# Seven products in place of eight for the gate and up projections of a SwiGLU block

## The chip, the cores and the metric

The kernel runs on one core of a Trainium2 chip. The metric is the device time of one execution in microseconds; the time of a kernel is the median of its runs. Each kernel also leaves one profiled execution, taken by the hardware profiler.

Engines by the names that the profile uses: PE is the matrix engine (PEld its weight loads), DVE the vector engine, ACT the scalar engine, POOL GpSimd, and SP the engine on whose queue the DMAs are issued. SBUF is the memory on the chip with 128 partitions, PSUM the eight banks of 128 x 512 floats into which PE accumulates, DRAM the memory outside.

## The reference

One layer of a bidirectional encoder on two sequences (prompt and sample) of 256 tokens each, so T = 512 columns in all, with a model width of 2048 and a feed-forward width of 5632, in float32:

```
hn = rms_norm(x, norm1_g) * (1 + sc1) + sh1          # sh, sc, gt: from silu(c) @ w_ada
h  = hn @ w_in                                       # RWKV-7 heads and a short convolution
x  = x + gt1 * (concat([y_rwkv, y_conv]) @ w_out)
hn = rms_norm(x, norm2_g) * (1 + sc2) + sh2
ff = (silu(hn @ w_ffn_gate) * (hn @ w_ffn_up)) @ w_ffn_down
y  = rms_norm(x + gt2 * ff, norm_f_g)
```

The change concerns the last three lines. sh2, sc2 and gt2 are vectors of 2048 for each of the two sequences; they come from a product of silu(c) with w_ada (2048 x 12288), which the kernel computes piece by piece beside other work.

## The kernel before

Everything is kept transposed: a row tile is 128 channels on the partitions and the 512 tokens as columns, the prompt in columns 0 to 255 and the sample in 256 to 511. KT = 16 row tiles make the model width, FT = 44 column tiles the feed-forward width.

**Precision.** A float32 product is made of three matmuls on a faster rounded format (fp32r): a weight is split into a high part (rounded, by ACT, `acopy`) and a low part (the rest, by DVE, `tt` with subtract), an activation likewise, and high x high, high x low and low x high are accumulated. `products` (L529) issues the three, `split` (L511) makes 512 columns of high and low weights, four 128 x 128 blocks, into one of four ring slots h. `load` (L522) brings 512 KB of raw weights (eight blocks) into one of three slots w. `stream` (L536) walks a list of tiles in this way, and `mtile` (L557) lists the products for one output tile of 512 columns in one bank.

**Order.** The code does not issue its instructions in the order written. `Program.add` records each operation with its engine, an estimated cost, what it reads and writes, and a priority; `Program.schedule` (L239) then plans the whole kernel, engine by engine, always taking the ready operation of the lowest priority number, and the instructions are issued in the planned order. Each engine's queue then runs strictly in that order, SP's DMA queue included. Priorities that matter here: 0 for weight splits (S_SPLIT), 1 for evacuations and most DMAs (S_EVAC), 5 for other side work (S_MISC), 8 for w_ada work (S_ADA), 9 for the large products (S_MAIN). Buffers are named slots: r0 to r15, g0 to g23, w0 to w2, h0 to h3, aw and aacc, each of 1024 columns. An operation that writes a slot under a new name waits for all earlier uses of it.

**The FFN.** After the out projection, `halves` (L1104) finishes its last four row tiles for the prompt columns first and then for the sample, so that the norm of one half runs beside the products of the other. `hn2_half` (L1174) makes the normalized activations hn2 of one row tile and one sequence, as high and low parts. The first three gate and up tiles run together over all row tiles (`head_tiles`), with their first four row tiles done by halves of 256 columns, their weights kept in six slots. Then for each further tile f, gate and up run as 16 x 3 matmuls of 512 columns each; `gate_done` applies silu from PSUM, `up_done` (L1208) multiplies and splits the result into one of twelve slots av. As soon as eleven activations (FCH) are there, the down projection adds their share to all 16 row tiles (four chunks, NCH): `down_done` (L1234) adds gt2 times the product to the residual x1 in SBUF. So gate, up and down alternate in four rounds:

```
nf = 3
for c in range(NCH):
    while nf < min(FCH * (c + 1) + 1, FT):
        for j in range(2):
            b0 = 2 * (2 * (nf - 3) + j)
            stream(lambda i, b0=b0: w_gu1[b0 + i],
                   mtile(hn2, next_bank(5), (gate_done, up_done)[j](nf)))
        nf += 1
```

The last four row tiles of the last chunk go by halves again, followed by the final norm.

**w_ada.** `ada_rest` (L758) brings one group of 512 columns of w_ada, in one of two ways. With slots it uses PE; without, it loads sixteen 256 KB pieces into the two halves of aw, and DVE multiplies and accumulates them into aacc (two operations of 512 columns each), before eight small matmuls sum over the partitions. Groups 12 to 15 (ADA_LATE), which give gt2, go the second way, written after the norm of the FFN.

## Time and profile before

| what | before |
| --- | --- |
| time, median of 3 runs | 2552.27 us (2551.53 to 2554.98) |
| profiled execution | 2558.41 us, span 2556.2 us |
| PE busy | 2493.4 us, 15340 matmuls |
| DVE busy | 1467.7 us, 2807 instructions |
| ACT busy | 969.8 us, 1764 instructions |
| DMA | 352.73 MB, 138 GB/s over the span |

The span runs from the first to the last instruction of the profiled execution; its whole time is a little longer. Matmuls are pipelined, and the duration of one matmul in the profile is longer than the distance to the next, so the rate is read from the starts in the timeline. Rows of the timeline give start, length, engine, line, operation, output and inputs by the program's names, and the count; idle time before the row and what ended it stand in square brackets. Rows of groups give busy time in us and the mean of one in ns after the first bar, idle time just before them and its causes after the second. The rows of 40 digits are busy tenths of 40 equal slices of the span.

### The profile page before, as it was taken

How to read it: one execution, taken by the hardware profiler on the slowest of the kernel's cores; microseconds unless marked ns; L12 is line 12 of the kernel's file. 1: busy time of each engine (PE TensorE's matmuls, PEld its weight loads, DVE VectorE, ACT ScalarE, POOL GpSimd, SP SyncE). 2: the span in 40 equal slices, each digit the busy share in tenths (PEclk: the TensorE clock that was granted, in tenths of full speed). 3: DMA queues.
4: the chain of work that ended last, by engine and by line, in shares of the span. 5: the costliest groups of instructions: out<-in, count | busy, mean ns of one | idle time of the engine just before them, and what ended most of it. 6: DMA issues, size and time to landing. Idle time of an engine off the chain costs nothing.

```text
span 2556.2 us, 39032 instructions
## 1 busy us (share of the span) xinstructions
PE 2493.4 (98%) x15340; PEld 1990.8 (78%) x15340; DVE 1467.7 (57%) x2807; ACT 969.8 (38%) x1764; POOL 12.5 (0%) x42
## 2 busy tenths in 40 slices
PE   6999999999999999999999999999999999999997
PEld 3578777777777777788788888888888888888887
DVE  4279988888988887888733333333333333333345
ACT  4474663754654732333222222222222222222232
POOL 0000000000000000000000000000000000000000
PEclk9999999999999999999999999999999999999999
DMA  9943443544544757636533333333333333333333
GB/s 347 362 145 122 145 135 113 147 130 128 154 132 126 239 185 266 206 124 191 182 98 99 91 99 99 94 96 99 93 97 99 99 93 98 99 93 98 99 93 105
DMA packets 147880, 352.73 MB, mean 138 GB/s; under 512 B 31856, under 2 KB 46576, under 8 KB 147696
## 3 DMA queue, kind: packets, MB, share of 16 engines
q1 hardware_dynamic: 147696, 350.24, 43.7%
q8 instruction: 120, 1.97, 0.3%
q14 instruction: 64, 0.52, 0.1%
HBM read 339.30 MB, written 12.45 MB: 138 GB/s over the span
## 4 chain that ended last, share of the span: by engine, by line
PE 82%; DVE 7%; DMA 6%; ACT 3%; issue 2%; SPq 1%; DVEq 0%; ACTq 0%
PE b L374 82%; DVE g L405 3%; DMA aw<-in_w_ada_dram 2%; ACT g L396 2%; DVE h L405 1%; DVE aacc L410 1%; DVE g L410 1%; DMA g<-hrmean 1%; SPq L438 1%; DMA g<-hrpre 1%; DMA w<-in_w_out_dram 0%; ACT h L396 0%; DVE r L410 0%; PE b L385 0%; ACT L396 0%
## 5 line engine op out<-in xcount | busy, mean ns | idle before, releaser
L374 PE MATMUL b<-r,h 128*128 128x512 f32 x4872 | 1187.6, 396 | 4.4 <-ACT r L396 1.9
L374 PEld LDWEIGHTS b<-r,h 128*128 128x128 f32 x4872 | 901.7, 189 | 223.8 <-issue 28.4
L374 PE MATMUL b<-g,h 128*128 128x512 f32 x4460 | 1045.0, 392 | 0.8 <-ACT g L396 0.5
L405 DVE TENSOR_TENSOR h<-w,h 128x512 fp32r<-128x512 f32 (+3 forms) x795 | 539.7, 680 | 784.1 <-ACT h L396 753.7
L374 PEld LDWEIGHTS b<-g,h 128*128 128x128 f32 x4460 | 836.1, 188 | 191.9 <-issue 11.2
L396 ACT ACTIVATE h<-w 128x512 fp32r<-128x512 f32 x787 | 492.8, 627 | 1237.9 <-PE b L374 1182.5
L410 DVE SCALAR_TENSOR_TENSOR aacc<-aw,sil,aacc 128x512 f32<-128x512 f32 x390 | 276.1, 744 | 60.1 <-DMA aw<-in_w_ada_dram 58.8
L405 DVE TENSOR_TENSOR g<-g,g 128x512 f32<-128x512 f32 (+24 forms) x699 | 255.9, 374 | 34.2 <-ACT g L396 12.2
L396 ACT ACTIVATE g<-b 32x128 f32<-32x128 f32 (+4 forms) x442 | 175.6, 402 | 133.1 <-PE b L374 101.3
L374 PEld LDWEIGHTS b<-g,g 128*64 128x64 f32 (+4 forms) x4104 | 158.8, 140 | 49.2 <-issue 27.2
L374 PE MATMUL b<-g,g 128*64 128x64 f32 (+4 forms) x4104 | 179.3, 229 | 4.4 <-DVE g L441 1.9
L396 ACT ACTIVATE g<-g 128x512 f32<-128x512 f32 (+3 forms) x190 | 113.7, 601 | 63.4 <-DVE g L405 52.3
L410 DVE SCALAR_TENSOR_TENSOR r<-b,md,r 128x256 f32<-128x256 f32 x192 | 84.9, 478 | 53.6 <-PE b L374 53.6
L405 DVE TENSOR_TENSOR g<-g,b 128x512 f32<-128x512 f32 x60 | 41.1, 685 | 59.4 <-PE b L374 59.3
L374 PE MATMUL b<-g,sil 128*32 128x512 f32 (+1 forms) x384 | 44.0, 554 | 21.0 <-DMA g<-in_w_ada_dram 19.1
L396 ACT ACT_TABLE_LOAD x45 | 57.7, 1283 | 1.5 <-PEq L1399 0.7
L405 DVE TENSOR_TENSOR g<-b,cs 64x256 f32<-64x256 f32 (+1 forms) x128 | 49.6, 416 | 1.8 <-PE b L374 0.2
L396 ACT ACTIVATE g<-r 128x512 f32<-128x512 f32 (+1 forms) x40 | 21.7, 543 | 49.5 <-DVE r L410 39.3
L374 PEld LDWEIGHTS b<-g,sil 128*32 128x32 f32 x384 | 9.3, 113 | 39.0 <-ACT g L396 17.6
L441 DVE STREAM_TRANSPOSE g<-g 128x512 f32<-128x512 f32 (+1 forms) x32 | 38.4, 1211 | 0.4
L396 ACT ACTIVATE g<-g,md 128x256 f32<-128x256 f32 (+1 forms) x48 | 25.1, 561 | 22.3 <-DVE md L405 12.7
L385 PE MATMUL b<-cs,g 128*128 128x128 f32 x160 | 23.0, 278 | 7.6 <-DVE g L405 6.4
(83 smaller groups left out, 559.4 us busy)
## 6 DMA issues: line engine op xcount, KB each, us to landing
w<-in_w_gu_dram SPq DMA_DIRECT2D x176, 512.0 KB
aw<-in_w_ada_dram SPq DMA_DIRECT2D x208, 256.0 KB
w<-in_w_in_dram SPq DMA_DIRECT2D x102, 512.0 KB
w<-in_w_down_dram SPq DMA_DIRECT2D x88, 512.0 KB
g<-in_w_ada_dram SPq DMA_DIRECT2D x80, 512.0 KB
w<-in_w_out_dram SPq DMA_DIRECT2D x32, 512.0 KB
g<-in_xT_dram SPq DMA_DIRECT2D x8, 512.0 KB
r<-in_xT_dram SPq DMA_DIRECT2D x16, 256.0 KB
```

Of the source, the lines that this page charges most:

```text
L374: return [nc.tensor.matmul(R(out), lhsT=R(l), rhs=R(r), start=start, stop=stop) for out, l, r, n, start, stop, one in mms]
L385: return [nc.tensor.transpose(R(out), R(i), R(idn)) for out, i, idn in items]
L396: lambda: nc.scalar.activation(out=R(out), in_=R(in_), func=func, scale=R(scale), bias=R(bias)),
L405: lambda: e.tensor_tensor(out=R(out), in0=R(a), in1=R(b), op=op), [a, b], [out], prio)
L410: lambda: e.scalar_tensor_tensor(out=R(out), in0=R(a), scalar=R(s), in1=R(b), op0=op0, op1=op1),
L438: add(eng, cost, lambda: e.dma_start(R(out), R(in_)), [in_, *after], [out], prio, nbytes=nbytes)
L441: add("dve", 0.37 if n == 256 else 0.05 + n / 560.0, lambda: nc.vector.transpose(R(out), R(in_)), [in_], [out], prio)
```

## The change

For the column tiles 4 to 43, gate and up are computed for pairs of column tiles (f, f + 1) and pairs of row tiles (x, y) at once. With the weights as a 2 x 2 block matrix (two column tiles by two row tiles) and the activations as another (two row tiles by two halves of 256 tokens), the 2 x 2 block product is made of seven block products instead of eight, by the Winograd form of Strassen's method. Each block product is again three fp32r matmuls, now of 256 columns.

- `make_u`, once for each of the eight pairs of row tiles, makes the four sums of activation blocks that the method needs, in place of the float32 copy of hn2 that `hn2_half` now also writes over x1, and splits them (four DVE operations of 256 columns, two of 512 and two of ACT), into slots ua and ub.
- `pair_weights` loads two pieces of 256 KB (four row tiles of two column tiles), forms four sums of weight blocks on DVE (512, 256 and 256 columns), and splits three plain blocks per row pair (768 columns) and the four sums (1024 columns). Its rings: four raw slots, two for the sums, two for each kind of part.
- `pair_products` runs this four times for a pair of column tiles and gate or up, with 42 matmuls each, into four banks: banks 4 to 7 for gate, 0 to 3 for up.
- `pair_sums` combines the seven results into the four output blocks (one ACT copy, five DVE operations of 256 columns and one of 512).
- The product of silu(gate) and up, two tiles at once, is stored to DRAM (actd). The down projection no longer alternates with gate and up, but comes as a stage of its own. Its four chunks load their eleven activations from DRAM and split them (`load_act`); the next chunk's are loaded while the current one runs.
- The residual x1 is stored to DRAM after the out projection (`save_x1`), because its slots are used for other things, and loaded again for the last chunk (`load_x1`). The down projection sums plainly (`acopy` for the first chunk, one DVE sum of 512 columns for the others), and gt2 and the residual are applied once at the end (`add_x1`).
- The late w_ada groups are written after the first chunk of down. Two slots (aw, aacc) take the place of g8 and g9 for the kept weights of the head.

```diff
     def out_done(m):
         def f(ps):
             gated_add(2, m)(ps)
+            save_x1(m)
             sumsq(x1[m], tmp(), sqa2, m == 0, S_EVAC)
...
     def hn2_half(k, q):
...
+        act(x1[k][:, s], t[:, s], AF.Identity, TQ, S_EVAC, bias=md[:, 3, k, q:q + 1])
...
-    for gi in ADA_LATE:
-        ada_rest(gi)
...
+    def make_u(j):
+        x, y = (x1[k] for k in rows_of(j))
+        b11, b12, b21, b22 = x[:, 0:TQ], x[:, TQ:T], y[:, 0:TQ], y[:, TQ:T]
+        tt(b11, b12, b11, ALU.subtract, TQ, S_MISC)
+        tt(b12, b22, b12, ALU.add, TQ, S_MISC)
+        tt(b22, b22, b11, ALU.add, TQ, S_MISC)
+        tt(b21, b21, b22, ALU.subtract, TQ, S_MISC)
+        for u, v in ((ua[j], x), (ub[j], y)):
+            acopy(u[:, 0:T], v, T, S_MISC)
+            tt(u[:, T:], v, u[:, 0:T].bitcast(F32), ALU.subtract, T, S_MISC)
...
+    ring_raw = ring(raws + [Slot.of["aw"]], F32)
+    ring_s = ring([Slot.of["aacc"], gs[23]], F32)
+    ring_parts = [ring(x) for x in (hls[0:2], hls[2:4], gs[16:18], r1s[14:16])]
...
+    def pair_weights(f, j, n):
+        x, y = ring_raw(), ring_s()
+        ha, la, hs, ls = (r() for r in ring_parts)
+        for a in range(2):
+            b = 2 * (2 * (f + 1 - a - 3) + j) + n // 2
+            dma(x[:, 512 * a:512 * a + 512], w_gu1[b][:, 512 * (n % 2):512 * (n % 2) + 512], 1 << 18, S_EVAC)
+        acopy(ha[:, 0:768], x[:, 256:1024], 768, S_SPLIT)
+        two256 = [128, 2, 256]
+        tt(y[:, 0:512].rearrange("p (a c) -> p a c", a=2), x[:, 0:256][:, None, :].to_broadcast(two256),
+           x[:, 256:768].rearrange("p (a c) -> p a c", a=2), ALU.subtract, 512, S_SPLIT)
+        tt(y[:, 512:768], x[:, 512:768], y[:, 0:256], ALU.subtract, 256, S_SPLIT)
+        tt(y[:, 768:1024], x[:, 768:1024], y[:, 512:768], ALU.subtract, 256, S_SPLIT)
+        acopy(hs, y, 1024, S_SPLIT)
+        tt(la[:, 0:768], x[:, 256:1024], ha[:, 0:768].bitcast(F32), ALU.subtract, 768, S_SPLIT)
+        tt(ls, y, hs.bitcast(F32), ALU.subtract, 1024, S_SPLIT)
...
+                    for (hi, lo), (ah, al), (b, c, end) in zip(ws[i][g_], xs, place[g_]):
+                        ps, stop = banks[b][:, TQ * c:TQ * c + TQ], bool(end) and k == KT // 2 - 1
+                        pe([(ps, hi, ah, TQ, k == 0 and b not in seen, False, True),
+                            (ps, hi, al, TQ, False, False, True), (ps, lo, ah, TQ, False, stop, True)], S_MAIN,
+                           after=[seen[b]] if k == 0 and b in seen else [])
...
+    for f in range(4, FT, 2):
+        pair_products(f, 0, bank[4:8])
+        pair_sums(bank[4:8], gate2)
+        act(gate2, gate2, AF.Silu, 2 * T, S_EVAC)
+        pair_products(f, 1, bank[0:4])
+        pair_sums(bank[0:4], up2)
+        tt(up2, up2, gate2, ALU.mult, 2 * T, S_EVAC)
+        for i in range(2):
+            dma(all_of(actd[f + i]), up2[:, T * i:T * i + T], 1 << 18, S_EVAC)
...
+    early = halves_of([Slot.of[n] for n in ("aw", "aacc")])
+    in_act, in_x1 = halves_of(r1s[14:16] + gs[16:17]), halves_of(gs[17:18] + by_pair[2 * FCH + 8:])
...
+    def load_act(c, i, after=()):
+        a = VT(place[c % 2][i], F32R).v()[:, 0:2 * T]
+        t = early.pop(0) if early else in_act[(FCH * c + i) % len(in_act)]
+        dma(t, all_of(actd[FCH * c + i]), 1 << 18, S_EVAC, after=after)
+        acopy(a[:, 0:T], t, T, S_EVAC)
+        tt(a[:, T:], t, a[:, 0:T].bitcast(F32), ALU.subtract, T, S_EVAC)
+        return a
...
     def down_done(c, m):
         def f(ps):
-            gated_add(5, m)(ps)
+            if c == 0:
+                acopy(x1[m], ps, T, S_EVAC)
+            else:
+                tt(x1[m], x1[m], ps, ALU.add, T, S_EVAC)
             if c == NCH - 1:
+                add_x1(m, 0, 2)
                 sumsq(x1[m], tmp(), sqa2, m == 0, S_EVAC)
+                load_x1(m + AHEAD, [x1[m]])
+            elif m < FCH:
+                coming.append(load_act(c + 1, m, [x1[m]]))
+            elif c == NCH - 2 and m >= KT - AHEAD:
+                load_x1(m - (KT - AHEAD), [x1[m]])
```

More of the change, by code (lines that the diff above doesn't have):

```diff
@@ L1102, in gated_half, with halves @@
         return f
-    def halves(blocks, acts, kind, tiles, last, slots, norm, at):
+    def halves(blocks, acts, done, tiles, last, slots, norm, at):
         kept = [VT(x, F32R).v() for x in slots]
@@ L1184, in norm2, with save_x1 @@
             hn2_half(k, q)
+    x1d = [Scratch(drp.tile([128, T], F32, name=f"x1d{m}")) for m in range(KT)]
+    def save_x1(m):
+        dma(all_of(x1d[m]), x1[m], 1 << 18, S_EVAC)
     at = {"i": 0}
@@ L1231, in hymba_layer_kernel, with ring, take @@
                 products(kept[i // 4][:, w:w + 128], kept[i // 4][:, 512 + w:640 + w], *t)
+    for j in range(KT // 2):
+        make_u(j)
     stream(lambda i: w_gu0[i], tiles, at=at)
+    for j in range(2):
+        stream(lambda i, j=j: w_gu1[2 * j + i], mtile(hn2, bank[j], (gate_done, up_done)[j](3)))
+    def ring(slots, dt=F32R):
+        v, n = [VT(s, dt).v() for s in slots], [0]
+        def take():
+            n[0] += 1
+            return v[(n[0] - 1) % len(v)]
+        return take
@@ new lines, in hymba_layer_kernel @@
+    raw0[:] = [VT(s).v() for s in raws]
+    tmpv = [VT(gs[i]).v() for i in (20, 21, 22)]
+    tmpq[:] = [tmpv[i // 2][:, T * (i % 2):T * (i % 2) + T] for i in range(6)]
+    sqa2 = VT(gs[23]).v()[:, T:]
+    bctr["n"] = 3
+    def load_act(c, i, after=()):
[5 more added lines that the diff above has]
+        return a
@@ new lines, in down_done, with down_half, f @@
+        return f
+    def down_half(m, q):
+        def f(ps):
+            s = slice(TQ * q, TQ * q + TQ)
+            tt(x1[m][:, s], x1[m][:, s], ps, ALU.add, TQ, S_EVAC)
+            add_x1(m, q, q + 1)
+            sumsq(x1[m][:, s], tmp()[:, s], sqa2[:, s], False, S_EVAC)
+            if q == 0:
+                load_x1(m + AHEAD, [x1[m][:, s]])
+        return f
+    acts = [load_act(0, i) for i in range(FCH)]
+    wide.update((n, VT(Slot.of[n]).v()) for n in ("aw", "aacc"))
+    for c in range(NCH):
+        tiles, last, coming = [], LAST_DOWN * (c + 1 == NCH), []
```

92 lines of the change are left out of this document (72 added, 20 removed).

## The prediction

> **What bounds the kernel now.** I read the page first, then the timeline of PE in the two FFN stages, then the timeline and groups of DVE and ACT there, then busy time by stretches. From the page: the span, TensorE and its granted clock, and the vector engine by slices.
>
> ```profile
> span 2556.2 us, 39032 instructions
> PE 2493.4 (98%) x15340; PEld 1990.8 (78%) x15340; DVE 1467.7 (57%) x2807; ACT 969.8 (38%) x1764; POOL 12.5 (0%) x42
> ...
> DVE  4279988888988887888733333333333333333345
> ...
> PEclk9999999999999999999999999999999999999999
> ```
>
> The chain of waits, in order of time, ends in one piece of TensorE work that covers the whole second half, followed by the last normalization on DVE:
>
> ```profile
> 1234.51 1306.48 PE b L374 x5885
> 2545.80 3.95 DVE g L410 x10
> ```
>
> So from 1234 us on nothing but the rate of matmuls sets the time. That rate comes from the timeline of TensorE in the gate and up stage (start, length, engine, line, operation, count); the next two rows are the same engine where the kernel before already multiplies by 256 columns instead of 512, first in the head of the FFN and then in the last chunk of the down projection:
>
> ```profile
> 1314.00 5.60 PE L374 MATMUL b<-r,h 128*128 128x512 f32 x24
> 1319.44 5.60 PE L374 MATMUL b<-g,h 128*128 128x512 f32 x24
> ...
> 1094.00 14.39 PE L374 MATMUL b<-r,g 128*128 128x256 f32 x120
> 1108.23 4.04 PE L374 MATMUL b<-r,h 128*128 128x512 f32 x17
> ...
> 2508.39 11.62 PE L374 MATMUL b<-g,r 128*128 128x256 f32 x96
> 2519.84 4.46 PE L374 MATMUL b<-g,g 128*128 128x256 f32 x36
> ```
>
> From start to start: 5.44 us for 24 is 226.7 ns for 512 columns; 14.23 us for 120 is 118.6 ns and 11.45 us for 96 is 119.3 ns for 256 columns. Half the columns thus cost 0.526 of the time, not 0.5. I take 119.3, since that stretch reads weights as they are split, as the new stage will.
>
> **The change: TensorE.** Per pair of row tiles, pair of column tiles and gate or up, the old code runs 8 block products of three matmuls over 256 columns, which it issues as 12 of 512. The new code runs 7 block products, 21 matmuls of 256. There are 20 pairs of column tiles (f = 4 to 42), two matrices and 8 pairs of row tiles: 320 units. Old: 320 x 12 x 226.7 ns = 870.5 us. New: 320 x 21 x 119.3 ns = 801.7 us. **Gain 68.8 us**, that is 1.72 us in each of 40 half pairs (21.76 us before, 20.04 us after). Of the 12.5% of columns saved, the shorter matmuls give back 4.6 points. With 118.6 ns it would be 73.5 us.
>
> A weight load now has to fit beside half as long a matmul. The busy time by stretches shows that it does, even with DVE full and the clock at 1.00:
>
> ```profile
> core 0: us, PE busy (x) PEld busy (x) DVE busy (x) ACT busy (x) POOL busy (x), PEclk, DMA share, GB/s
> 1094.00:1108.00 14.00, 14.00 (x122) 14.00 (x121) 14.00 (x37) 7.86 (x18) 0.00 (x0) 1.00 0.00 1
> ```
>
> The Trainium skill, TensorE: Matmul & The Clock Gate, section "The mechanism", speaks against this: weight loads are said to overlap running matmuls only where their row groups differ, and here all are 128 rows. The row disagrees: 120 loads and 120 matmuls went by at 118.6 ns a pair. What it would do to the time is a rival below.
>
> **DVE and ACT in the new stage.** Groups by shape, for the costs (count, busy us, mean ns), and two neighbouring starts in the timeline of DVE:
>
> ```profile
> L405 DVE TENSOR_TENSOR h<-w,h 128x512 fp32r<-128x512 f32 x403 | 278.6, 691 | 635.0 <-ACT h L396 612.4 <-PE b L374 22.6
> L396 ACT ACTIVATE h<-w 128x512 fp32r<-128x512 f32 x402 | 254.2, 632 | 781.1 <-PE b L374 777.6 <-issue 3.5
> ...
> L405 DVE TENSOR_TENSOR h<-w,h 128x256 fp32r<-128x256 f32 x8 | 3.3, 418 | 0.3 <-ACT h L396 0.2
> L396 ACT ACTIVATE h<-w 128x256 fp32r<-128x256 f32 x8 | 3.2, 406 | 0.0
> L405 DVE TENSOR_TENSOR g<-b,g 128x256 f32<-128x256 f32 x16 | 6.7, 416 | 4.0 <-PE b L374 4.0
> ...
> 1314.20 0.69 DVE L405 TENSOR_TENSOR g<-g,b 128x512 f32<-128x512 f32 x1 [1.59 <-PE b L374]
> 1314.80 0.68 DVE L405 TENSOR_TENSOR h<-w,h 128x512 fp32r<-128x512 f32 x1
> ```
>
> A tensor_tensor has 0.69 us at 512 columns and 0.42 at 256, so by their slope an estimate of 0.97 at 768 and 1.24 at 1024; followed by independent work the next one starts 0.09 us before the end (0.60 from start to start). ACT, in the same way: 0.86 at 768, 1.08 at 1024.
>
> pair_weights, once per eight weight blocks (two units, 42 x 119.3 ns = 5.01 us of TensorE): DVE 0.69 + 2 x 0.42 + 0.97 + 1.24 = 3.74 us; ACT 0.86 + 1.08 = 1.94 us. Four of these make a half pair: 14.96 us of DVE. pair_sums adds 5 x 0.42 + 0.69 = 2.77 us, the final product half of 1.24. So DVE takes **18.35 us of the 20.04** with nothing overlapped, and 15.97 with 0.09 off each of about 26.5 instructions: 80 to 92%. ACT: 7.76 + 0.4 + half of 1.08 = 8.7 us. Before, DVE was at 33% here, so the engine loses nearly all of its slack, but keeps enough. I cost it at nothing. The cover is depth: two sets of split weights are 10 us of matmuls, and the order lets DVE make the low part (0.97 us) while ACT rounds the sums (1.08 us). If that cover goes, see the second rival.
>
> **Loads.** A unit pair takes 512 KB in 5.01 us, 105 GB/s, as two DMAs of 2 KB rows; the stage before moved 98 GB/s:
>
> ```profile
> 1600.00:1800.00 200.00, 200.00 (x879) 164.75 (x878) 66.68 (x105) 52.39 (x84) 0.00 (x0) 1.00 0.33 98
> ...
> 1100.00:1200.00 100.00, 100.00 (x501) 83.53 (x501) 81.64 (x139) 32.25 (x55) 0.00 (x0) 1.00 0.54 167
> ```
>
> The second row holds many loads of the same 256 KB form (w_ada) at 167 GB/s for 0.54 of the DMA engines, the same 300 GB/s per full share as the first. The stores of activations add 13 GB/s, their reloads and x1 (60 x 256 KB over down's 64 tiles of 33 x 226.7 ns, 479 us) 33 GB/s. Four raw buffers give SP 15 us of lead. Nothing. What one DMA costs SP's queue, what one ACT write of 256 columns with a bias costs, and the longest wait in the chain for a 256 KB piece near here:
>
> ```profile
> L438 SPq DMA_DIRECT2D w<-in_w_gu_dram x128: 327/328/328, 1458.0 to 2391.6; - x128
> ...
> L396 ACT ACTIVATE r<-g,md 128x256 fp32r<-128x256 f32 x16 | 7.3, 501 | 12.3 <-DVE g L410 12.3
> ...
> 1218.23 4.34 DMA aw<-in_w_ada_dram
> ```
>
> **Start of the stage.** save_x1 puts 16 stores on SP's queue, each behind the sum it stores; behind them wait w_ada pieces and the first FFN weights. 32 more ACT writes of x1 (0.5 us each) lie behind the normalization, and make_u takes 8 x (4 x 0.42 + 2 x 0.69) = 24.5 us of DVE under some 87 us of matmuls (72 head tiles and 32 of f = 3, three matmuls each at 226.7 ns is 71 us, plus 17 of 256 columns). In exchange the four late w_ada groups leave this place. TensorE stalls here now:
>
> ```profile
> 1083.53 0.65 PE L374 MATMUL b<-aacc,cs 128*32 128x128 f32 x8 [2.68 <-DVE aacc L410]
> 1084.59 0.65 PE L374 MATMUL b<-aacc,cs 128*32 128x128 f32 x8 [0.41 <-DVE aacc L410]
> 1085.81 1.01 PE L374 MATMUL b<-cs,g 128*128 128x1 f32 x4 [0.57 <-DVE asum L441]
> 1087.78 0.58 PE L374 MATMUL b<-r,g 128*128 128x256 f32 x1 [0.96 <-ACT r L396]
> ...
> 1085.00:1090.00 5.00, 3.28 (x20) 2.67 (x12) 4.66 (x19) 1.48 (x5) 0.00 (x0) 0.50 0.32 107
> ```
>
> These 4.6 us of idling could go (-5), or the stores could delay what it waits for by as much as the 16 x 0.33 = 5.3 us of queue, with a colder clock after it (+8). I take 0, since its causes stay as they are.
>
> **The late w_ada groups** move into down chunks 0 to 2: 128 multiply-adds on DVE and 64 DMAs on SP. In order on DVE they wait for their DMAs, and weight splits stand behind them:
>
> ```profile
> L410 DVE SCALAR_TENSOR_TENSOR aacc<-aw,sil,aacc 128x512 f32<-128x512 f32 x119 | 84.5, 746 | 27.3 <-DMA aw<-in_w_ada_dram 27.1
> ```
>
> 128 x 0.746 = 95 us over about 360 us. A down tile is 7.48 us and needs of DVE 2.75 splits, one sum and 11/16 of an activation split, 3.1 us; with w_ada that is 68%. Four split buffers cover 10.9 us of matmuls, more than such a wait. Nothing; the groups' own matmuls only move.
>
> **From gate and up to down.** The eleven activations of chunk 0 come back from DRAM into buffers that the last products leave free: four early, four after the third quarter of the last half pair (5 us ahead), the rest after its end. An activation needs a DMA (4.3 us by the row above), 0.63 us of ACT and 0.69 of DVE; the first tile wants the ninth 8 x 3 x 0.227 = 5.4 us after the last product. pair_sums and the final product stand ahead on DVE (4 us). Bounds: 0, and 4.3 + 11 x 0.69 = 12 us if all come after the end, plus some 5 us at a clock near 0.5 as in the row above: 17 us. I take 2, near the lower end, since eight of eleven can be early.
>
> **End.** The tail gains one 256-column sum in front of the gated add (0.42 us); the last chunk's other sums lie under matmuls.
>
> Sum: -68.8 + 0 + 0 + 2 + 0.4 = **-66.4 us**. The profiled execution took 2558.4 us for its span of 2556.2; it becomes 2492.0. It lies 6.1 us above the median of the runs, 2552.3, which becomes **2486 us**.
>
> **Rivals.**
>
> *Round trip.* The mechanism holds, but the DRAM path opens stalls at both edges: 17 us at the start of down and 8 us at the start of FFN instead of my 2, so 2486 + 23 = 2509. For it: TensorE idled in this way around 1085 us. Against it: the loads are spread, and weights run ahead.
>
> *DVE behind ACT.* Each pair_weights is a chain: three DVE operations, ACT's rounding of the sums, the last subtraction. If the planned order leaves DVE idle during ACT's 1.08 us instead of doing the low part, a half pair takes 4 x (3.74 + 1.08) + 3.39 = 22.7 us. Idle time of over 0.42 us per pair_weights lengthens the stage, and at 0.85 the half pair is back at its old 21.76. With all 1.08 the time is 2552 + 40 x 0.91 + 2 = 2591 us, **slower**. For it: 92% in the unfavourable count, strict order on each engine. Against it: buffers two deep and other work ready to stand in the gap.
>
> *Weight loads pace TensorE.* If short matmuls cannot hide their loads once accumulators change every third matmul, the spacing is the load's own 0.188 us:
>
> ```profile
> L374 PEld LDWEIGHTS b<-g,h 128*128 128x128 f32 x3295 | 618.5, 188 | 133.4
> ```
>
> 6720 x 0.188 = 1263 us against 870, so 2945 us. That would follow from the Trainium skill's rule above. The 120 matmuls from 1094 on also change bank every third one, at 118.6 ns: nearly excluded.
>
> **How the numbers follow.** Forecast 0.75, with its own range 2476 (stalls at 1085 gone, 118.6 ns) to 2500; round trip 0.17; DVE behind ACT 0.06, of which a third ends below the old time; weight loads 0.01; gains just cancelled 0.01. No change means within 0.2%, 5 us, about what this measurement can tell. Faster 0.75 + 0.17 + 0.02 = 0.94, same 0.01, slower 0.05. The range takes in the forecast and most of the round trip: 2476 to 2512.
>
> **What would show it.** Right: a gate and up stage of about 802 us in 40 steps of 20 us, 256-column matmuls about 119 ns apart, DVE near 85% and clock 1.00 there, a gap of no more than a few us in TensorE before down. Wrong: idle PE inside the half pairs released by DVE's h, r or g (second rival), spacing over 125 ns with no idle time, or a gap of over 10 us at an edge.

## The result, and the profile after

The changed kernel takes 2481.61 us (median of four runs, 2476.94 to 2483.07) against 2553.14 us for the kernel before, measured beside it (four runs, 2551.53 to 2554.98). The ratio is 0.9716 with a 95% interval of 0.9700 to 0.9733, so the change gains 71.5 us. The prediction was 2486 us, a gain of 66.4. The profiled execution after took 2481.56 us, at the median; the one before lay 5 to 6 us above its median, so the two profiles differ by 76.9 us rather than 71.5.

From the page of the changed kernel, the same lines as were shown of the one before:

```profile
span 2479.7 us, 46341 instructions
PE 2418.7 (98%) x18220; PEld 2066.7 (83%) x18220; DVE 1911.8 (77%) x3511; ACT 1112.5 (45%) x1848; POOL 12.5 (1%) x42
...
DVE  4279988889889897795888888888888887734356
...
PEclk9999999999999999999999999999999999999998
```

The last pieces of its chain of waits (start, length, what it was):

```profile
1086.38 1066.37 PE b L374 x7994
2155.72 308.54 PE b L374 x1486
2469.53 3.12 DVE g L410 x8
```

TensorE still sets the end: the chain is one run of matmuls from 1086 us on, interrupted once, then the last normalization. DVE went from three tenths to eight tenths in the gate and up stage and did not enter the chain there. The granted clock is full as before.

The timeline of TensorE of the changed kernel (start, length, engine, line, operation, count) gives the new stage. The rows are the first matmuls of the head of the FFN, the last of 512 columns ahead of the new stage, the starts of the first, second and fifth group of 42 matmuls (the fifth opens the second half pair, up), and the last matmul of the stage with the first of the down projection behind it:

```profile
1105.96 16.51 PE L374 MATMUL b<-r,h 128*128 128x512 f32 x72
...
1171.27 5.60 PE L374 MATMUL b<-g,h 128*128 128x512 f32 x24
1176.71 0.88 PE L374 MATMUL b<-r,h 128*128 128x256 f32 x6
...
1181.69 0.88 PE L374 MATMUL b<-r,h 128*128 128x256 f32 x6
...
1196.64 0.88 PE L374 MATMUL b<-r,h 128*128 128x256 f32 x6
...
1974.18 0.28 PE L374 MATMUL b<-g,r 128*128 128x256 f32 x1
1974.30 1.55 PE L374 MATMUL b<-r,h 128*128 128x512 f32 x6
```

A group of 42 takes 1181.69 - 1176.71 = 4.98 us, a half pair 1196.64 - 1176.71 = 19.93 us, that is 118.6 ns per matmul, and the whole stage 1974.30 - 1176.71 = 797.6 us for 6720 matmuls, 118.7 ns each. Between the stage and down there is no gap: 0.12 us from the last start to the next is one matmul. Busy time by stretches, in two halves of that stage:

```profile
core 0: us, PE busy (x) PEld busy (x) DVE busy (x) ACT busy (x) POOL busy (x), PEclk, DMA share, GB/s
1176.00:1576.00 400.00, 400.00 (x3369) 399.85 (x3368) 339.42 (x529) 169.38 (x191) 0.00 (x0) 1.00 0.36 120
1576.00:1974.00 398.00, 398.00 (x3356) 398.00 (x3355) 337.77 (x526) 171.42 (x197) 0.00 (x0) 1.00 0.36 122
```

TensorE is never idle, the weight loads lie wholly beside the matmuls, DVE is at 85%, ACT at 43%, and the DMA engines at about a third.

Where the 76.9 us between the two profiles lie, from the first 512-column matmul of the FFN's head (1108.23 us before, 1105.96 after):

| part | before, us | after, us | difference |
| --- | --- | --- | --- |
| start of the head of the FFN | 1108.2 | 1106.0 | -2.3 |
| gate and up, column tiles 4 to 43 (before: 3840 matmuls at 226.7 ns) | 870.5 | 797.6 | -72.9 |
| the rest, from that start to the start of the last product | 562.0 | 560.4 | -1.6 |
| tail, and time outside the span | 17.7 | 17.6 | -0.1 |

The first row is taken as scatter: over all the kernels profiled below this start lies between 1099.7 and 1116.1 us, in no order that follows from their edits, and runs of one and the same kernel differ by nearly as much (2444.78 to 2457.51 us for the kernel wts64 below).

### The profile page after: what moved, and what is told of

Read it like the earlier page. It is cut to its first block, busy times and chain, and to the rows that moved or that the text cites. A ratio compares the mean times of both kernels' runs of the same rounds, so it can differ in the third digit from the quotient of the medians.

```text
span 2479.7 us, 46341 instructions
## 1 busy us (share of the span) xinstructions
PE 2418.7 (98%) x18220; PEld 2066.7 (83%) x18220; DVE 1911.8 (77%) x3511; ACT 1112.5 (45%) x1848; POOL 12.5 (1%) x42
## 4 chain that ended last, share of the span: by engine, by line
PE 86%; DVE 5%; DMA 5%; ACT 2%; issue 1%; SPq 0%; DVEq 0%; ACTq 0%
PE b L374 86%; DVE g L405 2%; DMA aw<-in_w_ada_dram 1%; ACT g L396 1%; DVE h L405 1%; DVE g L410 1%; DVE aacc L410 1%; DMA g<-hrvar 1%; DMA w<-in_w_out_dram 1%; PE b L385 1%; DMA g<-hrpre 1%; DMA w<-in_w_gu_dram 0%; DMA g<-hrmean 0%; ACT L396 0%; DMA hrmean<-rowm 0%
## 5 line engine op out<-in xcount | busy, mean ns | idle before, releaser
L374 PE MATMUL b<-r,h 128*128 128x512 f32 (+1 forms) x4920 | 1130.5, 375 | 4.8 <-ACT r L396 2.5
L396 ACT ACTIVATE h<-w 128x512 fp32r<-128x512 f32 (+2 forms) x587 | 391.8, 670 | 643.2 <-PE b L374 572.9
L374 PE MATMUL b<-g,h 128*128 128x256 f32 (+1 forms) x3452 | 654.1, 332 | 0.5 <-DVE rowp L418 0.2
L374 PEld LDWEIGHTS b<-g,h 128*128 128x128 f32 x3452 | 534.0, 190 | 73.8 <-issue 11.2
L374 PE MATMUL b<-g,g 128*128 128x256 f32 (+4 forms) x5372 | 427.2, 241 | 4.0 <-DVE g L405 2.9
L374 PEld LDWEIGHTS b<-g,g 128*128 128x128 f32 (+4 forms) x5372 | 354.1, 152 | 48.7 <-issue 25.6
L396 ACT ACTIVATE g<-g 128x1024 fp32r<-128x1024 f32 (+6 forms) x268 | 204.2, 763 | 247.0 <-DVE aacc L405 102.6
L374 PE MATMUL b<-r,g 128*128 128x256 f32 x1412 | 269.5, 283 | 1.5 <-ACT r L396 1.3
L374 PEld LDWEIGHTS b<-r,g 128*128 128x128 f32 x1412 | 214.2, 191 | 1.9 <-ACT r L396 1.4
L374 PE MATMUL b<-g,r 128*128 128x256 f32 x748 | 194.7, 281 | 0.0
```

The source lines that it names most:

```text
L374: return [nc.tensor.matmul(R(out), lhsT=R(l), rhs=R(r), start=start, stop=stop) for out, l, r, n, start, stop, one in mms]
L396: lambda: nc.scalar.activation(out=R(out), in_=R(in_), func=func, scale=R(scale), bias=R(bias)),
```

## The experiments

Two questions were tried: whether the stage is set by the number of matmuls alone and how much room the other engines have (the first six), and, when the spacing of matmuls turned out to be uneven, what sets it (the other six). All are edits of the changed kernel, except the last. Stage means gate and up from column tile 4 on, from its first matmul to the first of down; "head to last" runs from the start of the first 512-column matmul of the FFN to the start of the last product, which leaves out the scatter of the first 1100 us. It is 1432.5 us before and 1358.0 after (some expectations below give 1432.7 and 1358.2, which reach to the end of that product). Times without an interval are single runs.

### The eighth product

```diff
-        place = [[(0, 0, 0), (0, 1, 1), (1, 1, 0)], [(3, 0, 1), (2, 0, 0), (2, 1, 1), (1, 0, 1)]]
+        place = [[(0, 0, 0), (0, 1, 1), (1, 1, 0)], [(3, 0, 0), (2, 0, 0), (2, 1, 1), (1, 0, 1), (3, 1, 1)]]
```

The eighth block product repeats one set of weights, goes into the half bank that seven products leave free, and is not used by anything.

> Edit: in every unit of two row tiles by two column tiles an eighth block product is added to the seven (three more matmuls of 256 columns, into the half bank that was free); nothing reads its result. Theory A (the number of matmuls times 118.6 ns, as measured in the changed kernel, sets the stage): 320 units x 3 x 118.6 ns = 113.9 us more, so about 2596 us, slower than the kernel before by about 42 us, since eight products of 256 columns cost 24 x 118.6 = 2846 ns against 12 x 226.7 = 2720 ns. Theory B (the vector engine or the chain through ScalarE already paces the stage, and TensorE only fills it): a good part of the eighth product is hidden, so under 2560 us, and matmuls of 256 columns show gaps in the changed kernel that this one fills.

Measured: 2602.98 us, 1.0181 of the kernel before (1.0151 to 1.0211). The edges of the stage in its timeline of TensorE:

```profile
1181.12 0.88 PE L374 MATMUL b<-r,h 128*128 128x256 f32 x6
...
2091.66 0.28 PE L374 MATMUL b<-r,r 128*128 128x256 f32 x1
2091.78 1.55 PE L374 MATMUL b<-r,h 128*128 128x512 f32 x6
```

Its busy time in one stretch (TensorE, weight loads, DVE, ACT, POOL, clock, DMA):

```profile
1176.00:1576.00 400.00, 400.00 (x3355) 399.10 (x3353) 303.90 (x461) 147.89 (x167) 0.00 (x0) 1.00 0.33 105
```

The stage is 910.66 us for 7680 matmuls, 118.6 ns each, so 113.1 us more than with seven. With the same DVE work and eight products the change would have lost 47 us against the kernel before. The gain is the product left out, and short matmuls by themselves cost: 24 of 256 columns take 2.846 us, 12 of 512 took 12 x 226.7 ns = 2.720.

### Everything but the seven products

```diff
-    for f in range(4, FT, 2):
-        pair_products(f, 0, bank[4:8])
...
+    for f in range(4, FT):
+        for j in range(2):
+            stream(lambda i, f=f, j=j: w_gu1[2 * (2 * (f - 3) + j) + i],
+                   mtile(hn2, next_bank(5), (gate_done, up_done)[j](f)))
```

Gate and up go by 512 columns as before, with the residual and the activations through DRAM and down as a later stage.

> Edit: everything of the change is kept (residual and activations through DRAM, the down projection as a later stage, the sums of activation blocks) except the seven products: gate and up of column tiles 4 to 43 run again as 16 x 3 matmuls of 512 columns per tile. Theory A (the whole gain is in the products): gate and up take 3840 x 226.7 ns = 870.5 us in place of the 797.6 us of the changed kernel, so 2481.6 + 72.9 = 2554.5 us, within 4 us of the kernel before. Theory C (part of the gain comes from the new staging, say from TensorE stalls that it removes): 2545 us or less, and the products alone would be worth less than 64 us. If the staging costs something that the products pay for: over 2560 us.

Measured: 2560.42 us (ten runs) against 2556.34 (thirteen), 1.0018 (1.0008 to 1.0029). Head to last is 1432.3 us against 1432.5 before. So the DRAM path and the new order cost next to nothing where they act; about 2 us of cost could hide there, since down now meets slow places in two chunks instead of four (see "Where the operands lie"). The 4 us on the whole then lie mostly outside this stretch; whether the copies of x1 or chance put them there isn't settled. By the interval, the staging costs at most 7.4 us.

### More work for DVE

```diff
         tt(ls, y, hs.bitcast(F32), ALU.subtract, 1024, S_SPLIT)
+        tt(y[:, 0:1024], x[:, 0:1024], y[:, 0:1024], ALU.add, 1024, S_SPLIT)
```

One more operation in each pair_weights, its result unused; the second kernel does it with 512 columns.

> Edit: one more vector operation of 1024 columns per pair_weights, behind the last subtraction (it adds into the buffer of sums, whose values are no longer needed), so the result is unchanged. Theory A (TensorE bounds as long as the vector engine's own work fits in a half pair of 19.93 us): from start to start such an operation costs about 1.14 us, four per half pair, so the vector engine goes from the 17.0 us per half pair that the changed kernel shows (339 of 400 us busy) to 21.5 us and becomes the bound: 40 x (21.5 - 19.9) = +64 us, about 2546 us, more if gaps behind ScalarE add to it (up to 2590). Theory B (the stage is paced by the chain through ScalarE, and each vector operation adds its full length): 160 x 1.14 = +182 us, about 2664 us.

> Edit: as with 1024 columns, but the extra vector operation per pair_weights has 512 columns; the result is unchanged. With 1024 columns the vector engine was busy without a pause and a half pair took 20.6 us, so its own work is 20.6 - 4 x 1.14 = 16.0 us of 19.93. Theory A: 512 columns cost 0.60 us from start to start, so 16.0 + 2.4 = 18.4 us, under 19.93: the pair stage keeps its 797.6 us, time within 3 us of 2481.6. If vector work costs TensorE time long before the engine is full (the chain through ScalarE): 160 x 0.6 = 96 us more.

Measured with 1024 columns: 2500.62 us, the stage 819.64 us. Its busy time in a stretch:

```profile
1370.00:1570.00 200.00, 194.44 (x1632) 193.57 (x1631) 199.66 (x298) 79.84 (x93) 0.00 (x0) 1.00 0.35 116
```

Two neighbouring pieces of its chain of waits:

```profile
1869.69 39.98 PE b L374 x335
1910.88 39.99 PE b L374 x335
```

All waits of TensorE from 1200 to 1950 us (total, times, longest):

```profile
PE b L374 <- ACT g L396: 16.7, 15, 1.1
PE b L374 <- DVE g L405: 0.4, 1, 0.4
```

DVE is full, and TensorE waits in nearly every pair of column tiles once, 1.1 us. This pair takes 1910.88 - 1869.69 = 41.19 us, a half pair 20.6 (20.5 in the mean of the stage). A subtraction of 1024 columns takes 1.13 us from start to start (1258.08 to 1259.21 us in the changed kernel's DVE timeline, shown below), so DVE's own work for a half pair is 20.6 - 4 x 1.13 = 16.1 us of the 19.93 that TensorE needs. DVE did become the bound, as theory A says, but the stage grew by 22 us and not by 64: the expectation took the 17.0 us that DVE is shown busy for its work, but where operations follow each other without a pause the next starts before the end of the one ahead, and the same work takes 16.1.

With 512 columns: 2483.78 us, the stage 797.59 us, and no wait of TensorE in the same stretch, though DVE is nearly full:

```profile
1370.00:1570.00 200.00, 200.00 (x1687) 200.00 (x1687) 191.82 (x306) 84.10 (x95) 0.00 (x0) 1.00 0.38 120
```

The edge of DVE's room therefore lies between these two, where 16.1 us of own work puts it: 3.8 us per half pair.

### One set of split weights

```diff
-    ring_parts = [ring(x) for x in (hls[0:2], hls[2:4], gs[16:18], r1s[14:16])]
+    ring_parts = [ring(x) for x in (hls[0:1], hls[2:3], gs[16:17], r1s[14:15])]
```

> Edit: one set of split weights in place of two in the pair stage (each of the four rings of parts has one slot). It takes away the cover that I named for the vector engine's work. The sums' parts of the next step can then be written only after the last product of this step: ScalarE 1.06 us, the vector engine 1.22 and some 0.25 between engines are 2.5 us, against 18 x 118.6 ns = 2.1 us of products that can run meanwhile; so at least 0.4 us of idle TensorE in each of 160 steps, 64 us: 2546 us, and up to 1 us each (2640 us) if other vector work stands in the way. If the two sets cover nothing (TensorE would have run just as well): 2482 us.

Measured: 2526.97 us; the stage 838.24 us, 40.6 us longer, or 0.25 us for each of 160 pair_weights. In its timeline the loss stands at the change from the plain blocks' products to those of the sums; the row with 18 matmuls is the first kind, the second and third row hold the pause:

```profile
1399.85 2.32 PE L374 MATMUL b<-g,h 128*128 128x256 f32 x18
1402.00 0.40 PE L374 MATMUL b<-r,g 128*128 128x256 f32 x2
1402.30 0.38 PE L374 MATMUL b<-r,r 128*128 128x256 f32 x1
1402.52 0.39 PE L374 MATMUL b<-g,g 128*128 128x256 f32 x2
```

1402.00 to 1402.52 us is 0.52 us for three matmuls that should take 0.36; this pause is 0.16 us, of a mean of 0.25. So the second set is real cover and is worth 40.6 us, but not the 64 or more expected. ACT and DVE at the same place (the rounding of the next sums, and their low part):

```profile
1399.93 1.06 ACT L396 ACTIVATE g<-g 128x1024 fp32r<-128x1024 f32 x1 [2.14 <-PE b L374]
1401.02 1.23 DVE L405 TENSOR_TENSOR r<-g,g 128x1024 fp32r<-128x1024 f32 x1 [1.45 <-ACT g L396]
```

The two kinds of parts have rings of their own. ACT writes the rounded sums anew right behind their last matmul (1399.73 us), beside the 18 matmuls of the plain blocks, and the first matmul that needs the new low part starts at 1402.30 us, right behind DVE's end at 1402.25. The chain has the length that was expected, some 2.5 us, but 20 matmuls cover it and not 18, since the first two of the sums need only the rounded part. The rest of the pause, 0.10 us behind that matmul, stays unexplained.

### Activations of the first down chunk late

```diff
-    acts = [load_act(0, i) for i in range(FCH)]
+    acts = [load_act(0, i, [up2]) for i in range(FCH)]
```

All eleven loads now wait for the last product to be written.

> Edit: the eleven activations of the first down chunk are loaded only after the last product of gate and up is written, in place of as soon as their buffers are free. It puts a price on the bound of my second rival (17 us). ScalarE and the vector engine need about 4.5 us for the last sums and product, then a DMA (2.5 to 4.3 us), 0.63 and 0.69 us until the first matmul of down: 8 to 10 us of idle TensorE, then activations every 0.69 us against 0.68 us of matmuls each, and a colder clock for a few us: 10 to 17 us more, 2492 to 2499 us.

Measured: 2494.88 us; head to last 1372.4 us, 14.4 longer. TensorE at the edge:

```profile
1981.19 3.23 PE L374 MATMUL b<-r,h 128*128 128x512 f32 x6 [7.92 <-ACT r L396]
1984.92 0.49 PE L374 MATMUL b<-r,h 128*128 128x512 f32 x1 [0.50 <-ACT r L396]
1985.64 0.73 PE L374 MATMUL b<-r,h 128*128 128x512 f32 x2 [0.23 <-DVE r L405]
```

8.65 us idle, and the first six matmuls stretched from 1.55 to 3.23 us; the granted clock is 0.50 from 1981 to 1984 us. Down starts 8.1 us later behind the first matmul of the stage, and its first nine matmuls lose 2.9 more, so the edge itself costs 11 us. The other 3.3 us come at waits for the late w_ada groups, the first 45 us into down. Kernels with other edits show such waits too (dve512 below, under "Loads"), so this part can't be put down to the late loads alone. The prediction's upper bound for this edge, 17 us, was too high by half, but of the right kind; the early loads save all of the 11 us in the changed kernel.

### Where the operands lie

In the timeline of the changed kernel, down runs at two rates. Starts in its second and third chunk (start, length, count):

```profile
2160.97 2.20 PE L374 MATMUL b<-r,h 128*128 128x512 f32 x9
...
2168.45 2.20 PE L374 MATMUL b<-r,h 128*128 128x512 f32 x9
...
2239.49 1.55 PE L374 MATMUL b<-g,h 128*128 128x512 f32 x6
...
2247.09 1.55 PE L374 MATMUL b<-g,h 128*128 128x512 f32 x6
```

One tile of 33 matmuls takes 7.48 us in the one (226.7 ns) and 7.60 in the other (230.3 ns), with TensorE busy and at full clock in both. What differs is the slots that the activations come from. By the order in which the program places its slots, and because g14 has 1040 columns of four bytes, five slots (g15 to g19) lie 64 bytes further from a multiple of 128 than the rest: at 96 instead of 32 bytes past it. Two of those, g16 and g17, hold the high parts of the weight sums in the new stage. Six kernels change only where slots lie; nothing is added or taken away. The first puts all at a multiple of 128 bytes, the second all but g16 and g17 at 32:

```diff
-    row_pre, row_fin, row_bon, row_mean = const("rowp", 64), const("rowf", 64), const("rowb", 128), const("rowm", 128)
+    row_pre, row_fin, row_bon, row_mean = const("rowp", 64), const("rowf", 88)[:, 0:64], const("rowb", 128), const("rowm", 128)
...
-    for s in low + hls[2:4] + r1s + gs[0:20]:
+    for s in low + hls[2:4] + r1s + gs[0:14] + gs[15:20] + gs[14:15]:
```

> Edit: no instruction is changed; 96 bytes are added to a constant and the one slot of 1040 columns is placed last, so that all slots of 1024 columns start at a multiple of 128 bytes in each partition. In both kernels they start at 32 modulo 128, except g15 to g19, which start at 96. In the down projection's chunks whose activations lie partly in g15 to g19 (all four before, the first and third after) the matmuls of 512 columns come every 229.5 to 230.5 ns, elsewhere every 226.7. Theory D (what costs is that a matmul's operands lie at unequal places modulo 128): the slow chunks go to 226.7 ns: 2 x 528 x 3.8 ns = 4 us less, 2477.6 us. Theory E (any start that is not a multiple of 64 or 128 bytes costs, also the 32 of all slots): besides, 512 columns come nearer to the 213.3 ns that they need at the granted clock of 1.00 and 2.4 columns per ns, up to 13 ns less for each of some 8000 and 10 ns for each of some 7000 shorter matmuls: 100 us or more. Theory F (the place doesn't matter): 2481.6 us.

```diff
-    for s in low + hls[2:4] + r1s + gs[0:20]:
+    for s in low + hls[2:4] + r1s + gs[0:14] + gs[15:16] + gs[18:20] + gs[14:15] + gs[16:18]:
```

> Edit: places only. Of the five slots that start at 96 modulo 128, the two that hold the rounded sums of weights (g16, g17) stay there; g15, g18 and g19 go to 32 like the rest. With all slots alike, the down projection ran at 226.7 ns throughout, but the seven products at 120.0 ns in place of 118.6, and it was the products with g16 and g17 as weights that had been faster (117.7 against 120.0). Theory G (weights that lie 64 bytes off the activations are loaded or swapped sooner; activations that lie off cost): pair stage as in the changed kernel, 797.5 us or a little less, down chunks all at 226.7, so 4 us less than the changed kernel from the head of the FFN to the last product (1354 us against 1358.2). Theory H (the gain in the pair stage came from g18 and g19, the first two of eight sums of activations): pair stage 806 us, as with all slots alike. The whole time can't tell 4 us from the scatter of the first 1100 us; the length of the stages in the trace can.

The third puts all slots of split weights at 32 and all slots of activations at 96:

```diff
-    hls = [Slot(f"h{i}", gp, 1024) for i in range(4)]
+    hls = [Slot(f"h{i}", gp, 1040 if i == 3 else 1024) for i in range(4)]
...
-    for s in low + hls[2:4] + r1s + gs[0:20]:
+    for s in hls + low[2:] + r1s[0:14] + gs[0:14] + gs[15:16] + gs[18:20] + gs[14:15] + r1s[14:16] + gs[16:18]:
```

> Edit: places only. Every slot that holds weights (h0 to h3, r14, r15, g16, g17) starts at 32 modulo 128, every slot that holds activations at 96. Theory G (weights 64 bytes off the activations are faster, by 3.4 ns where all of them are): 256 columns at 116.6 ns or less, 783 us for the pair stage; if it holds for 512 columns too, 223 ns, and 30 us less over the FFN. Theory I (what counts is the step from one operand to the next of the same kind: a stream whose weights all lie alike runs at 120.0 and 226.7 wherever they lie): pair stage 806 us, down at 226.7 throughout.

| kernel | median, us (runs) | of before | stage, us | ns per matmul there | head to last, us |
| --- | --- | --- | --- | --- | --- |
| after | 2481.61 (4) | 0.9716 (0.9700 to 0.9733) | 797.6 | 118.7 | 1358.0 |
| align128 | 2481.76 (4) | 0.9704 (0.9684 to 0.9724) | 806.4 | 120.0 | 1362.8 |
| mix | 2479.68 (4) | 0.9702 (0.9689 to 0.9715) | 797.9 | 118.7 | 1357.4 |
| wts64 | **2449.86** (5) | **0.9580** (0.9565 to 0.9594) | **761.6** | **113.3** | 1323.2 |
| off64 (below) | 2473.87 (5) | 0.9670 (0.9656 to 0.9685) | 791.5 | 117.8 | 1348.3 |

Two neighbouring starts of a group of 42, from the timeline of the first (align128):

```profile
1172.99 0.88 PE L374 MATMUL b<-r,h 128*128 128x256 f32 x6
...
1178.02 0.88 PE L374 MATMUL b<-r,h 128*128 128x256 f32 x6
```

The same of the third (wts64):

```profile
1187.53 0.84 PE L374 MATMUL b<-r,h 128*128 128x256 f32 x6
...
1192.29 0.84 PE L374 MATMUL b<-r,h 128*128 128x256 f32 x6
```

And a stretch of the third, with the columns as above:

```profile
1188.00:1948.00 760.00, 760.00 (x6709) 760.00 (x6707) 668.30 (x1052) 339.80 (x386) 0.00 (x0) 1.00 0.39 127
```

5.03 us against 4.76 for the same 42 matmuls. In align128 down runs at 226.7 ns throughout, as theory D says, but the new stage grows by 8.8 us, which no theory had, and the time stays. In mix, the products of the sums, whose rounded weights lie in g16 and g17, run at 117.7 ns and all others at 120.0; the average is the changed kernel's 118.7. The 4 us expected of mix from head to last came out as 0.6: its down does run at 226.7 ns, but TensorE waits 2.0 us for late w_ada groups there and then runs at a granted clock of 0.74 (2155 to 2160 us). So where weights and activations lie sets the spacing, and with the third layout all 6720 matmuls take 113.3 ns. DVE does the same work in less time, 88% busy, and TensorE still never waits in the stage. This version is the best of all and beats both kernels: 0.958 of the kernel before, its median 31.8 us below the changed kernel's, and 34.8 us less from head to last.

The fourth kernel moves the split weights through all offsets in steps of 16 bytes, one offset for each pair of column tiles (20 pairs, so the series runs two and a half times), and by tiles in down. Its slots are larger, so the places of the h slots against each other differ too.

```diff
...
-        ha, la, hs, ls = (r() for r in ring_parts)
+        o = 4 * ((f - 4) // 2 % 8)
+        ha, la, hs, ls = (r()[:, o:o + 1024] for r in ring_parts)
```

> Edit: places only. All slots start alike modulo 128 bytes, and the slots of weights are 32 columns longer, so that the split weights can lie 0, 16, 32, ... or 112 bytes into them: in the pair stage the place goes up by 16 bytes with every pair of column tiles (20 pairs, eight places in turn), in the down projection with every 20 splits (240 matmuls of 512 columns). With weights 64 bytes off the activations the kernel before this one had 113.3 ns for 256 columns (120.0 with all alike) and 228.9 ns for 512 (226.7 with all alike). Theory G (the distance between weights and activations modulo 128 sets it): 120.0 at 0, 113.3 at 64, other values between or below; 512 columns 226.7 at 0, 228.9 at 64, and other distances show whether any goes below 226.7. Theory J (only multiples of 64 count, or only the absolute place): two values at most, one for 0 to 48 and one for 64 to 112. If it is not the place but something else in the last kernel: 120.0 in all pairs.

Measured: 2488.05 us, a single run. ns per matmul in the stage, the same each time an offset came round again:

| bytes | 0 | 16 | 32 | 48 | 64 | 80 | 96 | 112 |
| --- | --- | --- | --- | --- | --- | --- | --- | --- |
| ns | 119.2 | 118.7 | 119.1 | 117.9 | **113.4** | 117.8 | 117.4 | 119.9 |

It is no slope but one good place, and theory J's two values are not there. Offset 0 should have given 120.0 and 226.7 ns by theory G, since all lie alike within 128 bytes then; it gave 119.2 with 256 columns, and in the head of the FFN, where the offset is still 0, 72 matmuls of 512 columns take 16.65 us (231 ns each) against 16.35 in the changed kernel. In down the eight offsets gave 229 to 233 ns, all worse than the 226.7 of align128.

The fifth is the mirror image of the third: activations at 32, weights of the new stage at 96, and down's weights left alike with its activations.

```diff
+        ha, la = ha[:, 16:784], la[:, 16:784]
```

(Also r14, r15, g16 and g17 are placed behind g14, so that they lie 64 bytes further too.)

> Edit: places only. All slots start alike modulo 128, but what the pair stage uses as weights lies 64 bytes further: r14, r15, g16 and g17 are placed so, and the plain parts use columns 16 to 783 of h0 to h3 in place of 0 to 767. The 512-column matmuls keep weights and activations alike. Theory G from the runs before (weights 64 bytes off: 113.3 ns for 256 columns, but 228.9 for 512; alike: 120.0 and 226.7): pair stage 761.6 us, down projection back to 226.7 ns, 453 to 456 us; head of the FFN to the last product about 1319 us against 1358.0 in the changed kernel and 1323.2 with all weights off. Time 2481.6 - 39 = 2443 us, some 5 us less than with all weights off. If the pair stage stays at 797 us, the places of r14 to g17 relative to h0 to h3 had made the gain.

Neighbouring starts of a group of 42 in its timeline:

```profile
1178.70 0.87 PE L374 MATMUL b<-r,h 128*128 128x256 f32 x6
...
1183.64 0.87 PE L374 MATMUL b<-r,h 128*128 128x256 f32 x6
```

4.94 us, and over the whole stage 117.8 ns and not 113.3: down is back at 226.7 ns as expected, but the time is 2473.87 us and not 2443. The mirror image is not as good, so a difference of 64 bytes between weights and activations is not the whole rule. In the sixth, the kernel before has all its slots at multiples of 128 bytes:

```diff
-    row_pre, row_fin, row_bon, row_mean = const("rowp", 64), const("rowf", 64), const("rowb", 128), const("rowm", 128)
+    row_pre, row_fin, row_bon, row_mean = const("rowp", 64), const("rowf", 88)[:, 0:64], const("rowb", 128), const("rowm", 128)
...
-    for s in low + hls[2:4] + r1s + gs[0:20]:
+    for s in low + hls[2:4] + r1s + gs[0:14] + gs[15:20] + gs[14:15]:
```

> Edit of the kernel before, places only: all slots start at a multiple of 128 bytes. There the four down chunks ran at 229.5 ns per matmul of 512 columns, with activations partly in g15 to g19, which lay 64 bytes off; gate and up at 226.7. Theory D: down at 226.7 throughout, 4 x 528 x 2.8 ns = 5.9 us less from the head of the FFN to the last product (1426.8 us against 1432.7). If 229.5 stays, the cause lies elsewhere (the down weights, or the sums that are updated meanwhile).

Measured: 2547.56 us, 0.9960 of the kernel before (0.9946 to 0.9974); its matmuls of 512 columns are 226.7 ns apart throughout, down included, and head to last falls from 1432.5 to 1425.9 us. So the kernel before also paid for its layout, 6.6 us from head to last; the rest of the 11 us between the medians lies outside this stretch, where starts scatter.

## Why the prediction was right

**TensorE.** The term that carries the sum was 320 units x 21 matmuls x 119.3 ns. The count held, and that it is the count was shown twice: the eighth product costs 113.1 us, and without the seven products nothing remains of the gain. The spacing came out as 118.7 ns, nearer to the other row, 118.6 from 1094 us on, which was shown and not taken; that is 4.1 of the 4.4 us by which 2486 was too high. The reason given for taking 119.3 was misread and was not what sets it: in the stretch of the 119.3, from 2508.39 us on, the last split ends at 2509.04 us, and placing operands moves the same matmuls from 113.3 to 120.0 ns with the same splitting beside them. That the spacing came out so near is in part luck: the prediction had no term for the place of the slots, and 113.3 to 120.0 ns for 6720 matmuls are 45 us.

**DVE and ACT at nothing: right, with the sizes.** Groups by shape of the changed kernel in its stage, first DVE (count, busy us, mean ns, idle time before and what ended it):

```profile
L405 DVE TENSOR_TENSOR h<-w,h 128x768 fp32r<-128x768 f32 x119 | 113.4, 953 | 0.0
L405 DVE TENSOR_TENSOR r<-aacc,g 128x1024 fp32r<-128x1024 f32 x80 | 97.8, 1223 | 60.3 <-ACT g L396 60.3
L405 DVE TENSOR_TENSOR r<-g,g 128x1024 fp32r<-128x1024 f32 x79 | 96.5, 1222 | 48.0 <-ACT g L396 48.0
```

The same for ACT:

```profile
L396 ACT ACTIVATE h<-w 128x768 fp32r<-128x768 f32 x119 | 100.9, 848 | 88.0 <-PE b L374 67.1 <-DMA w<-in_w_gu_dram 17.5 <-DMA aw<-in_w_gu_dram 2.2
L396 ACT ACTIVATE g<-aacc 128x1024 fp32r<-128x1024 f32 x79 | 83.8, 1061 | 129.2 <-PE b L374 127.2 <-DVE g L405 2.0
```

Three rows of its DVE timeline:

```profile
1247.72 1.23 DVE L405 TENSOR_TENSOR r<-g,g 128x1024 fp32r<-128x1024 f32 x1 [1.29 <-ACT g L396]
...
1258.08 1.22 DVE L405 TENSOR_TENSOR r<-g,g 128x1024 fp32r<-128x1024 f32 x1
1259.21 0.68 DVE L405 TENSOR_TENSOR g<-g,b 128x512 f32<-128x512 f32 x1
```

The estimates by slope, 0.97 and 1.24 us on DVE, 0.86 and 1.08 on ACT, measured 0.953 and 1.223, 0.848 and 1.061. Of the two counts for a half pair, 15.97 us with overlap and 18.35 without, the first is the rate: 16.1 by the 1024-column experiment. The second is the sum of durations, and of use only for busy time.

**The rival of DVE behind ACT** names something that happens. DVE does stand idle for ACT's rounding of the sums, 1.29 us in the row above and 108 us in 159 operations, or 0.68 us for each pair_weights. By the prediction's own point, 0.42 us, that should have lengthened the stage. It didn't, because the point was reckoned from the count of 18.35: with 16.1, four times 0.68 us still fits into 19.93. And when more work was given to DVE, this idle time went (199.66 us busy of 200). Idle time on an engine that has room is no sign of a chain.

**Weight loads** do not pace TensorE at their own 0.188 us, as that rival had it: each of the 6720 short matmuls has its own load of 128 rows, the spacing is 118.7 ns, and the stretches show loads and matmuls busy together throughout. Whether the loads set a few ns of the spacing is open: the sweep of offsets moves the weights alone, and the spacing follows. The Trainium skill (TensorE: Matmul & The Clock Gate, "The mechanism") says in one line that loads overlap running matmuls only where row groups differ, and in another that a load into a background weight buffer is pulled ahead as well. Here loads of all 128 rows overlap, so the measurement decides against the first line taken alone; it can't tell about the second.

**Loads, the late w_ada groups, the first edge.** In the new stage and all of down, TensorE has a single wait:

```profile
PE b L374 <- DVE aacc L410: 1.0, 1, 1.0
```

It is one of the small matmuls of a late w_ada group, at 2155.72 us. "Nothing" for these groups was right to 1 us in this profile, but with some luck: in dve512, whose down is not changed, TensorE waits 2.8 us for them, runs at a granted clock of 0.72 from 2160 to 2165 us behind it, and takes 4.7 us longer from head to last with a stage of the same length. At the start of the FFN the stalls stayed. They were 4.6 us; the timeline of TensorE after shows them in square brackets:

```profile
1079.56 0.43 PE L374 MATMUL b<-aacc,cs 128*32 128x128 f32 x8 [0.34 <-DVE aacc L410]
1081.93 0.43 PE L374 MATMUL b<-aacc,cs 128*32 128x128 f32 x8 [1.94 <-DVE aacc L410]
1083.67 0.61 PE L374 MATMUL b<-cs,g 128*128 128x1 f32 x4 [1.32 <-DVE asum L441]
1085.61 0.58 PE L374 MATMUL b<-r,g 128*128 128x256 f32 x1 [1.33 <-ACT r L396]
```

0.34 + 1.94 + 1.32 + 1.33 = 4.9 us. The 0 was right, between -5 and +8.

**From gate and up to down** was put at 2 us and is 0 in the changed kernel. In eight and single, which leave down as it is, its first 30 matmuls lose 1.3 and 2.5 us, so the 2 was a fair price. The rival of the round trip, 23 us at two edges, has its mechanism, as the late loads show with 11 us at one of them, but the early slots keep it from acting. **The end** was put at 0.4 us; the added sum delays the gated add by 0.46 us, but the tail as a whole did not grow (the last row of the table above).

In sum: the profiles differ by 76.9 us where 66.4 were forecast. Of these 10.5 us, 4.1 are the spacing, 2 the edge, 2.3 the scattered start of the head and 0.5 the tail. The last 1.6 are the rest of the FFN, where two chunks of down instead of four meet slow places; by their spacing (4 x 528 x 2.8 ns against 2 x 528 x 3.8) that is worth 1.9 us.

## What to carry to other kernels

Where one engine is the bound from end to end and the others have room, a change of algorithm that takes instructions from that engine is worth their number times their spacing, and the cost of the extra work elsewhere is read from starts, not from durations. Before such a trade, look for the spacing of the smaller instruction in the same trace: 256 columns took 0.523 of 512, which turned an eighth into 8.4%. And look at where the operands lie: here the place of the slots was worth nearly half as much as the algorithm (34.8 us against 72.9 in the FFN), on top of it.

## What the runs showed of the hardware

The spacing of matmuls with a weight load each depends on where weights and moving operand lie in their partition, at full granted clock and with TensorE never waiting. With 256 columns it is 120.0 ns where all lie at the same place within 128 bytes (at 0 in align128, and at 32 in the plain blocks' products of mix, so the place itself does not count there), 117.8 where the weights lie at 96 and the activations at 32, and 113.3 where the weights lie at 32 and the activations at 96. With 512 columns it is the other way: 226.7 ns where all are alike (align128, before_alike), 228.9 with the layout that is best for 256, and up to 233 in the sweep of offsets. At 113.3 ns a short matmul is exactly half a long one, and the stage takes 761.6 us, seven eighths of 870.5.

The place within 128 bytes is not the whole rule. The slots of the sweep differ from those of the other kernels by multiples of 128 bytes, and at its offset 0, where all lie alike, it gave 119.2 and 231 ns in place of 120.0 and 226.7; so larger distances count too.

Open are the mechanism, why the two directions differ, why the sweep found its 113.4 ns at an offset of 64 bytes while the mirrored layout with that same difference gave 117.8 (its slots were spaced differently), and why long matmuls lose where short ones gain. The mirrored layout was meant to serve both lengths at once; it kept the 226.7 ns of the long matmuls but not the 113.3 of the short ones. The third layout for the new stage, with weights and activations alike in down, was not tried.
